# First stage of a two-block network on one core: loads chained tile by tile, four loads moved behind them, mean squares closed per stream, scale slices placed one feature tile later

## The chip, the core and the metric

The kernel runs on one core of one Trainium2 chip. The metric is the device time of one launch in microseconds; lower is better. TensorE is the matrix engine, VectorE (DVE in the rows) and ScalarE (ACT) do elementwise work, GpSimd (POOL) does little here, SyncE (SP) issues nearly all loads. Sixteen DMA engines carry what any of the queues issues.

## The reference, cut to what matters

The function is a chain of two network blocks on 256 tokens of width 1024, with a context of 256 more tokens. Only the beginning of the first block is touched by the change:

```python
mod = jax.nn.silu(c) @ w_mod[i] + b_mod[i]
sh1, sc1, ga1, sh2, sc2, ga2 = [m[:, None, :] for m in jnp.split(mod, 6, axis=-1)]
mod_c = jax.nn.silu(c_ctx) @ w_mod[i] + b_mod[i]
...
hc = modulate(ctx, g_mix[i], csh1, csc1)     # rmsnorm(ctx) * g * (1 + scale) + shift
hx = modulate(x, g_mix[i], sh1, sc1)
y, yc = mlstm_mixer(hx, hc, ...)             # k = hc, hx @ w_in[:, keys], gates, then q, v, o
```

So: root-mean-square norm of ctx and of x over their rows, a scale and a shift per feature that come from two vector-by-matrix products (one condition vector for each stream), and then the products of both streams with the key and gate columns. Everything after that (the rest of the first mixer, a gated convolution, and a second block with four feed-forward layers, a gated linear attention and a latent attention) is left as it is.

## The kernel before

A program lists all instructions in an order of the author's; a planner then places them on the engines by priority (earlier in the program goes first, `urgent()` raises a priority) as their inputs become ready in its own estimate. `behind(op, first)` tells it to place `op` behind `first` on the queue, without a semaphore. Buffers come from pools; a load whose buffer isn't free waits at its issue, and what stands behind it on that queue waits as well.

The first stage, `start()`, works on feature tiles f = 0 to 7 of 128 features each.

- Ahead of it, SP's queue loads ccol (both condition vectors as columns), ident, ctx into xc (two halves of 128 tokens), x (two halves), wsc0 (the scale weights of tile 0) and cols (small vectors), lines 138 to 151.
- `cond_rows()` (L482) spreads the condition vectors over all partitions by TensorE (L488), for the sums against the shift weights; VectorE and ScalarE copy the result (L490).
- Lines 499 to 505: the mean squares of the four halves, the first 512 columns of each on ScalarE (`mean_square`, L324), the second 512 on VectorE (L504). Line 507 closes all four at once and `rsqrt_half` (L295 to 319) takes the inverse root by integer arithmetic and three steps, ten small VectorE instructions with line 507.
- `features(h)` (L510): normalises columns h*512 to h*512+511 of both streams into xn (L517 on VectorE, L521 on ScalarE), turns them over on TensorE (L528) and copies the result to xt (L530). `features(0)` is urgent; `features(1)` stands after tile 0's products.
- `vectors(f)` (L545): loads wsc (scale weights of tile f, 512 KB) and wsh (shift weights, 512 KB), loads and splits the key and gate columns a_kg of the tile (`unit`, 320 KB; whi on ScalarE L236, wlo on VectorE L237), multiplies wsc with ccol on TensorE into pg (L556), sums wsh against each condition row on VectorE (`ttr`, L256) and closes gsc (scale, L563) and shc (shift, L566). From f = 3 on the pg matmuls stand behind the last product of tile f-3 (L558).
- `keys(f)` (L568): u = xt * gsc + shc for both streams on ScalarE (L572), split into a high and a low half (L245 and L576 on ScalarE, L246 on VectorE), and thirty-odd matmuls (L585 to L592) that accumulate keys and gates over the tiles. For tile 0 the high parts of both streams go through one matmul each (L585).

The program calls `vectors(0)`, `vectors(1)`, then for each f `vectors(f+1)` and `keys(f)`.

The scale weights and the high halves share eight buffers, the shift weights and the low halves another eight, and the raw loads five. Four more loads are called far later in the program, on POOL's queue: mpos (L664, 128 KB), gain (`row_load`, L400, 512 KB after it is spread over the partitions), gout (L1020, 128 KB) and perm (L1173, 64 KB). POOL's queue is empty at the start and their buffers are free, so the planner has put them first there.

## Time and profile before

| | us |
|---|---|
| median of three runs | 1430.35 |
| lowest and highest of the three | 1429.79, 1434.51 |
| the profiled execution | 1434.38 |
| its span, first to last instruction | 1432.6 |

Engines over the span: TensorE busy 1380.0 us (96%), VectorE 1113.9 us (78%), ScalarE 720.5 us (50%). The times in the rows are microseconds from the start of the span; "idle before <-" names what an engine waited for. [...] Ends of matmuls are modelled, so neighbours overlap in the rows.

### The profile page before, as it was taken

The numbers are of one execution on the slowest core, as the hardware profiler recorded it, in microseconds if no ns is written. First come the engines' busy times: TensorE is split into PE (matmuls) and PEld (weight loads), VectorE is DVE, ScalarE is ACT, GpSimd is POOL, SyncE is SP. The second block draws the span as 40 slices with busy tenths as digits, with TensorE's granted clock in tenths as the row PEclk, the third lists the DMA queues.
The fourth block names the chain that finished last, engine by engine and source line by source line (L and its number), as shares of the span: only waits on it lengthen the run. The fifth ranks groups of instructions, "written<-read, shape, count | busy, mean of one in ns | idle before, by whom it ended". The sixth has DMA issues, their size and how long they took to land.

```text
span 1432.6 us, 22526 instructions
## 1 busy us (share of the span) xinstructions
PE 1380.0 (96%) x8425; PEld 1204.0 (84%) x8425; DVE 1113.9 (78%) x2115; ACT 720.5 (50%) x1188; POOL 18.2 (1%) x42
## 2 busy tenths in 40 slices
PE   6999999999989999999999999999999999899997
PEld 6978877899978999878678999879999776789996
DVE  6887788898688888689788888698878786756563
ACT  4634764545354545566454545554554666644451
POOL 1000000000000000000000000000000000000000
PEclk8999999999999999999999999999999999999999
DMA  8576446797528999568548999469889472366750
GB/s 330 203 265 234 162 151 234 264 323 272 184 96 290 336 340 345 196 222 290 187 154 289 341 335 344 147 202 334 317 310 333 138 253 80 121 198 205 276 170 30
DMA packets 94943, 340.24 MB, mean 238 GB/s; under 512 B 10928, under 2 KB 11248, under 8 KB 94832
## 3 DMA queue, kind: packets, MB, share of 16 engines
q1 hardware_dynamic: 92736, 332.47, 65.6%
q0 software_dynamic: 2096, 6.33, 1.5%
q8 instruction: 66, 1.08, 0.3%
q14 instruction: 45, 0.37, 0.1%
HBM read 337.67 MB, written 1.08 MB: 236 GB/s over the span
## 4 chain that ended last, share of the span: by engine, by line
PE 70%; DVE 11%; DMA 10%; ACT 4%; issue 3%; SPq 0%; DVEq 0%; ACTq 0%; POOLq 0%
PE mm L250 12%; PE mm L252 11%; PE mm L251 11%; PE acc L252 8%; PE acc L250 8%; PE acc L251 8%; DMA raw<-in_cond_w_dram 3%; DVE wlo L237 3%; DVE gjunk L256 2%; PE acc L733 2%; ACT whi L236 1%; ACT ajunk L324 1%; PE pt L347 1%; PE pg L556 1%; DMA row<-d 1%
## 5 line engine op out<-in xcount | busy, mean ns | idle before, releaser
L237 DVE TENSOR_TENSOR wlo<-raw,whi 128x1024 fp32r<-128x1024 f32 (+1 forms) x385 | 462.5, 1207 | 109.6 <-ACT whi L236 106.7
L236 ACT CAST whi<-raw 128x1024 fp32r<-128x1024 f32 (+1 forms) x385 | 395.7, 1038 | 277.1 <-PE mm L251 79.5
L250 PE MATMUL mm<-u_hi,whi 128*128 128x256 f32 x1384 | 388.5, 281 | 0.2 <-DVE hf L831 0.2
L251 PE MATMUL mm<-u_lo,whi 128*128 128x256 f32 x1384 | 386.6, 279 | 0.0
L252 PE MATMUL mm<-u_hi,wlo 128*128 128x256 f32 x1384 | 386.5, 279 | 0.0
L250 PEld LDWEIGHTS mm<-u_hi,whi 128*128 128x128 f32 x1384 | 260.0, 188 | 4.4 <-DVE hf L831 0.6
L251 PEld LDWEIGHTS mm<-u_lo,whi 128*128 128x128 f32 x1384 | 259.3, 187 | 3.3
L252 PEld LDWEIGHTS mm<-u_hi,wlo 128*128 128x128 f32 x1384 | 260.1, 188 | 0.0
L256 DVE CUSTOM_DVE_ANT_0 gjunk<-raw,c 128x1024 bf16<-128x1024 f32 x192 | 234.3, 1221 | 24.1 <-DMA raw<-in_cond_w_dram 16.5
L250 PE MATMUL acc<-whi,hh 128*128 128x512 f32 x388 | 153.6, 398 | 4.5 <-ACT hh L245 4.5
L252 PE MATMUL acc<-whi,hl 128*128 128x512 f32 x388 | 153.3, 397 | 0.3 <-DVE hl L246 0.3
L251 PE MATMUL acc<-wlo,hh 128*128 128x512 f32 x388 | 152.5, 393 | 0.5 <-DVE wlo L237 0.5
L252 PEld LDWEIGHTS acc<-whi,hl 128*128 128x128 f32 x388 | 73.4, 189 | 17.4 <-DVE hl L246 0.7
L250 PEld LDWEIGHTS acc<-whi,hh 128*128 128x128 f32 x388 | 72.9, 188 | 17.5 <-ACT hh L245 5.0
L252 PE MATMUL acc<-whi,u_lo 128*128 128x512 f32 (+1 forms) x216 | 86.7, 403 | 0.5 <-DVE u_lo L246 0.5
L250 PE MATMUL acc<-whi,u_hi 128*128 128x512 f32 (+1 forms) x216 | 86.5, 401 | 0.0
L251 PE MATMUL acc<-wlo,u_hi 128*128 128x512 f32 (+1 forms) x216 | 86.4, 400 | 0.0
L251 PEld LDWEIGHTS acc<-wlo,hh 128*128 128x128 f32 x388 | 73.2, 189 | 14.2 <-DVE wlo L237 1.3
L251 PE MATMUL mm<-wlo,u_hi 128*128 128x512 f32 x144 | 57.3, 398 | 0.0
L250 PE MATMUL mm<-whi,u_hi 128*128 128x512 f32 x144 | 57.2, 397 | 0.0
L252 PE MATMUL mm<-whi,u_lo 128*128 128x512 f32 x144 | 57.0, 397 | 0.0
L946 ACT ACTIVATE sg<-mm 128x256 f32<-128x256 f32 x64 | 24.3, 380 | 59.6 <-PE mm L252 59.5
(734 smaller groups left out, 1998.6 us busy)
## 6 DMA issues: line engine op xcount, KB each, us to landing
raw<-in_cond_w_dram SPq DMA_DIRECT2D x144, 512.0 KB, 5.2
raw<-in_gu_ws_dram SPq DMA_DIRECT2D x128, 512.0 KB, 5.0
raw<-in_dn_dram SPq DMA_DIRECT2D x88, 512.0 KB, 4.9
raw<-in_gu_dram SPq DMA_DIRECT2D x48, 512.0 KB, 4.3
raw<-in_w_mod_dram SPq DMA_DIRECT2D x32, 512.0 KB, 4.3
raw<-in_f_down_dram SPq DMA_DIRECT2D x22, 512.0 KB, 4.6
raw<-in_f_gate_dram SPq DMA_DIRECT2D x18, 512.0 KB, 4.9
raw<-in_a_vo_dram SPq DMA_DIRECT2D x16, 512.0 KB, 5.1
```

Of the source, the lines that this page charges most:

```text
L236: o1 = S.copy(hi[:, :n], r[:, :n])
L237: o2 = V.tensor_tensor(out=lo[:, :n], in0=r[:, :n], in1=hi[:, :n].bitcast(F32), op=ALU.subtract)
L250: T.matmul(ps, lhsT=lh, rhs=rh, start=first, stop=False)
L251: T.matmul(ps, lhsT=lh, rhs=rl, start=False, stop=False)
L252: T.matmul(ps, lhsT=ll, rhs=rh, start=False, stop=last)
L256: return V.tensor_tensor_reduce(out=junk, in0=r, in1=vec, scale=1.0, scalar=0.0, op0=ALU.mult, op1=ALU.add, accum_out=dst)
L324: mark["ms"] = S.activation(out=junk[:, :src.shape[-1]], in_=src, func=AF.Square, scale=float(2 * width) ** -0.5, accum_out=dst)
L347: T.transpose(pt[:, k, :], src[:, (h * 4 + k) * 128:(h * 4 + k + 1) * 128], ident)
L556: o = T.matmul(pg, lhsT=wsc[:, k * 128:k * 128 + 128], rhs=ccol[:, k, :], start=(k == 0), stop=(k == 7))
L733: T.matmul(np_[:, 0:257], lhsT=w[:, d, s, :], rhs=vt[s][:, h, :], start=(i == 0), stop=(i == len(tiles) - 1))
L946: S.activation(out=sg, in_=ps[:, 0:256], func=AF.Silu)
```

## The change

Six edits, all in the first stage but for the four loads.

1. wsh of tile 0 is loaded with wsc of tile 0, ahead of cols.
2. The loads of the later tiles run in a chain: each key slice, wsc and wsh is placed behind the one before on SP's queue (`load`, `mark["loads"]`), in the order a_kg 0, wsc 1, wsh 1, a_kg 1, and so on.
3. mpos, gain, gout and perm go to SP's queue, behind the last load of that chain (`late`).
4. The mean squares are closed for each stream by itself, ctx first, and ctx's first features follow at once (`stats`, then `features(0, ...)`, both urgent). Instead of one closing chain for four values there are two for two values.
5. For the first half of x's tokens both column halves are squared on ScalarE; for the second half of x's tokens VectorE's square is placed behind ctx's scaling (`xn0`).
6. The pg matmuls of tile f stand behind the last product of tile f-2 rather than f-3, from f = 2 on.

```diff
--- before.py
+++ after.py
@@ -140,12 +140,14 @@
     nc.sync.dma_start(out=ident, in_=a["ident"])
     x = const.tile([128, 2, D], F32, name="x")
     wsc0 = hi_p.tile([128, 1024], F32, name="wsc", tag="w")
+    wsh0 = lo_p.tile([128, 1024], F32, name="wsh", tag="w")
     xc = ar.tile([128, 2, D], F32, name="xc", tag="A")
     for t in range(2):
         nc.sync.dma_start(out=xc[:, t, :], in_=a["ctx"][t * 128:(t + 1) * 128])
     for t in range(2):
         nc.sync.dma_start(out=x[:, t, :], in_=a["x"][t * 128:(t + 1) * 128])
     nc.sync.dma_start(out=wsc0, in_=a["w_sc"][0])
+    nc.sync.dma_start(out=wsh0, in_=a["w_sh"][0])
 
     cols = const.tile([128, LINE(NCOLS)], F32, name="cols")
     nc.sync.dma_start(out=cols[:, :NCOLS], in_=a["cols"])
@@ -177,9 +179,9 @@
     mod2 = const.tile([128, 20, 8], F32, name="mod2")
 
 
-    def raw_load(src):
+    def raw_load(src, load=nc.sync.dma_start):
         r = raw_p.tile([128, 1024], F32, name="raw", tag="raw")
-        nc.sync.dma_start(out=r[:, :src.shape[-1]], in_=src)
+        load(out=r[:, :src.shape[-1]], in_=src)
         return r
 
     pins, bg_pins, mark = [], [], {}
@@ -224,9 +226,9 @@
     def first(stage, i, src, slot=None):
         return early.pop((stage, i)) if (stage, i) in early else unit(src, slot)
 
-    def unit(src, slot=None):
+    def unit(src, slot=None, load=nc.sync.dma_start):
         n = src.shape[-1]
-        r = raw_load(src)
+        r = raw_load(src, load)
         if slot is None:
             hi = hi_p.tile([128, 1024], F32R, name="whi", tag="w")
             lo = lo_p.tile([128, 1024], F32R, name="wlo", tag="w")
@@ -395,9 +397,13 @@
         G.dma_start(out=r, in_=d.rearrange("a b -> (a b)").partition_broadcast(128))
         return r
 
-    def row_load(src):
+    def late(out, in_):
+
+        behind(nc.sync.dma_start(out=out, in_=in_), mark["loads"])
+
+    def row_load(src, load=G.dma_start):
         r = row_p.tile([128, D], F32, name="row", tag="row")
-        G.dma_start(out=r[:, :src.shape[-1]], in_=src.partition_broadcast(128))
+        load(out=r[:, :src.shape[-1]], in_=src.partition_broadcast(128))
         return r
 
     def acc_ps(t, h):
@@ -495,67 +501,81 @@
         V.tensor_scalar(out=b1, in0=col("b_mod", 8, 8), scalar1=1.0, scalar2=None, op0=ALU.add)
         xt = [ar.tile([128, 8, 256], F32, name=f"xt{i}", tag="BC"[i]) for i in range(2)]
         ss = sm.tile([128, 2, 4], F32, name="ss4", tag="ss4", bufs=1)
+        r2 = []
         cond_rows()
-        for i, src in ((0, xc), (1, x)):
+
+        def stats(i, src):
+
             for t in range(2):
                 j = i * 2 + t
                 mean_square(src[:, t, 0:512], ss[:, 0, j:j + 1], D)
+                if j == 2:
+                    mean_square(src[:, t, 512:1024], ss[:, 1, j:j + 1], D)
+                    continue
                 junk = wk.tile([128, D], BF16, name="gjunk", tag="gjunk", bufs=1)
-                V.tensor_tensor_reduce(out=junk[:, 0:512], in0=src[:, t, 512:1024], in1=src[:, t, 512:1024], scale=0.5 / D,
-                                       scalar=0.0, op0=ALU.mult, op1=ALU.add, accum_out=ss[:, 1, j:j + 1])
+                o = V.tensor_tensor_reduce(out=junk[:, 0:512], in0=src[:, t, 512:1024], in1=src[:, t, 512:1024],
+                                           scale=0.5 / D, scalar=0.0, op0=ALU.mult, op1=ALU.add, accum_out=ss[:, 1, j:j + 1])
+                if i:
+                    behind(o, mark["xn0"])
+            js = slice(i * 2, i * 2 + 2)
+            V.scalar_tensor_tensor(out=ss[:, 0, js], in0=ss[:, 0, js], scalar=0.5 * EPS, in1=ss[:, 1, js], op0=ALU.add, op1=ALU.add)
+            r2.append(rsqrt_half(ss[:, 0, js], 2))
+
+        def features(h, i, src):
+
+            xn = wk.tile([128, 2, 512], F32, name="xn", tag="xn")
+            for t in range(2):
+                w, r = src[:, t, h * 512:h * 512 + 512], r2[i][:, t:t + 1]
+                if t == 0:
+                    o = V.tensor_scalar_mul(out=xn[:, t, :], in0=w, scalar1=r)
+                    if h == 0:
+                        mark["xn"] = mark["xn0"] = o
+                else:
+                    o = S.activation(out=xn[:, t, :], in_=w, func=AF.Copy, scale=r)
+                    if h == 0:
+                        mark["xa"] = o
+            for t in range(2):
+                pt = (acc_ps(i, t) if h == 0 else mm_ps() if t == 0 else
+                      ps_tr.tile([128, 512], F32, name="pt", tag="tc")).rearrange("p (k n) -> p k n", k=4)
+                for k in range(4):
+                    T.transpose(pt[:, k, :], xn[:, t, k * 128:k * 128 + 128], ident)
+                dst = xt[i][:, h * 4:h * 4 + 4, t * 128:t * 128 + 128]
+                (S.copy if t else V.tensor_copy)(dst, pt)
+
+        streams = ((0, xc), (1, x))
         with urgent():
-            V.scalar_tensor_tensor(out=ss[:, 0, :], in0=ss[:, 0, :], scalar=0.5 * EPS, in1=ss[:, 1, :], op0=ALU.add, op1=ALU.add)
-            r4 = rsqrt_half(ss[:, 0, :], 4)
-
-        def features(h):
-
-            for i, src in ((0, xc), (1, x)):
-                xn = wk.tile([128, 2, 512], F32, name="xn", tag="xn")
-                for t in range(2):
-                    w, r = src[:, t, h * 512:h * 512 + 512], r4[:, i * 2 + t:i * 2 + t + 1]
-                    if t == 0:
-                        o = V.tensor_scalar_mul(out=xn[:, t, :], in0=w, scalar1=r)
-                        if h == 0:
-                            mark["xn"] = mark["xn0"] = o
-                    else:
-                        o = S.activation(out=xn[:, t, :], in_=w, func=AF.Copy, scale=r)
-                        if h == 0:
-                            mark["xa"] = o
-                for t in range(2):
-                    pt = (acc_ps(i, t) if h == 0 else mm_ps() if t == 0 else
-                          ps_tr.tile([128, 512], F32, name="pt", tag="tc")).rearrange("p (k n) -> p k n", k=4)
-                    for k in range(4):
-                        T.transpose(pt[:, k, :], xn[:, t, k * 128:k * 128 + 128], ident)
-                    dst = xt[i][:, h * 4:h * 4 + 4, t * 128:t * 128 + 128]
-                    (S.copy if t else V.tensor_copy)(dst, pt)
-
-        with urgent():
-            features(0)
+            for st in streams:
+                stats(*st)
+                features(0, *st)
         gsc = const.tile([128, 8, 2], F32, name="gsc")
         shc = const.tile([128, 8, 2], F32, name="shc")
         gp = mm_ps()
         kp = []
         kgu = {}
 
-        def kg_unit(f):
+        def load(out, in_):
+
+            o = nc.sync.dma_start(out=out, in_=in_)
+            if "loads" in mark:
+                behind(o, mark["loads"])
+            mark["loads"] = o
+
+        def vectors(f):
+
+            wsc, wsh = wsc0, wsh0
+            if f:
+                wsc = hi_p.tile([128, 1024], F32, name="wsc", tag="w")
+                load(wsc, a["w_sc"][f])
+                wsh = lo_p.tile([128, 1024], F32, name="wsh", tag="w")
+                load(wsh, a["w_sh"][f])
             if f < 1:
                 pin(1, 4)
-            kgu[f] = unit(a["a_kg"][f])
-
-        def vectors(f):
-
-            wsc = wsc0
-            if f:
-                wsc = hi_p.tile([128, 1024], F32, name="wsc", tag="w")
-                nc.sync.dma_start(out=wsc, in_=a["w_sc"][f])
-            wsh = lo_p.tile([128, 1024], F32, name="wsh", tag="w")
-            nc.sync.dma_start(out=wsh, in_=a["w_sh"][f])
-            kg_unit(f)
+            kgu[f] = unit(a["a_kg"][f], load=load)
             pg = ps_tr.tile([128, 2], F32, name="pg", tag="tr")
             for k in range(8):
                 o = T.matmul(pg, lhsT=wsc[:, k * 128:k * 128 + 128], rhs=ccol[:, k, :], start=(k == 0), stop=(k == 7))
-                if k == 0 and f >= 3:
-                    behind(o, mark["kg"][f - 3])
+                if k == 0 and f >= 2:
+                    behind(o, mark["kg"][f - 2])
             o = ttr(wsh, cc, shc[:, f, 0:1])
             if f == 0:
                 behind(o, mark["xn0"])
@@ -599,7 +619,8 @@
                 vectors(f + 1)
             keys(f)
             if f == 0:
-                features(1)
+                for st in streams:
+                    features(1, *st)
         return gp, kp
 
     gp, kp = start()
@@ -661,7 +682,7 @@
             gc = const.tile([128, 6, 64], F32, name="gc", tag="cc")
             V.tensor_copy(gc, gt_ps[:, 0:384].rearrange("p (s n) -> p s n", s=6))
         mpos = const.tile([128, 2, 128], F32, name="mpos", tag="cb")
-        G.dma_start(out=mpos, in_=a["mpos"])
+        late(out=mpos, in_=a["mpos"])
 
 
         qT = ar.tile([128, H, 256], F32, name="qT", tag="Q")
@@ -685,7 +706,7 @@
                 dst = vt[i][:, g * 2:g * 2 + 2, 0:256]
                 (S.copy if i % 2 else V.tensor_copy)(dst, flat[i].rearrange("p (h n) -> p h n", h=2))
                 site()
-        gain = row_load(a["a_gain"])
+        gain = row_load(a["a_gain"], late)
         so = scratch(0).rearrange("p (t n) -> p t n", t=2)
         for g in range(2):
             units = [unit(a["a_vo"][2 + g, j]) for j in range(4)]
@@ -1017,7 +1038,7 @@
         vt = scratch(0).rearrange("p (t n) -> p t n", t=2)
         rt = scratch(1).rearrange("p (t n) -> p t n", t=2)
         gout = hp.tile([128, 256], F32, name="gout", tag="gout", bufs=1)
-        G.dma_start(out=gout, in_=a["gl_gout"].partition_broadcast(128))
+        late(out=gout, in_=a["gl_gout"].partition_broadcast(128))
         units, got = {}, {}
 
         def vr(i, t):
@@ -1170,7 +1191,7 @@
         V.tensor_scalar(out=kf, in0=kf, scalar1=-1.0, scalar2=1.5707963267948966, op0=ALU.mult, op1=ALU.add)
         S.activation(out=mla.C, in_=kf, func=AF.Sin)
         mla.perm = const.tile([128, 128], F32, name="perm")
-        G.dma_start(out=mla.perm, in_=a["perm"])
+        late(out=mla.perm, in_=a["perm"])
 
     def rope(src, dst, tokens, rp):
```

## Rows read from the trace of the kernel before

**Rows 1.** The page: the chain that ended last, share of the span by engine.

```profile
PE 70%; DVE 11%; DMA 10%; ACT 4%; issue 3%; SPq 0%; DVEq 0%; ACTq 0%; POOLq 0%
```

**Rows 2.** Windows: stretch, length, busy us of each engine (instructions), PEclk, DMA share, GB/s.

```profile
14.20:20.90 6.70, 6.35 (x30) 6.38 (x31) 4.68 (x19) 2.50 (x5) 0.00 (x0) 0.50 1.03 403
20.90:24.40 3.50, 2.65 (x24) 2.48 (x22) 3.50 (x9) 3.25 (x7) 0.00 (x0) 0.99 1.02 408
24.40:31.20 6.80, 5.53 (x21) 5.14 (x22) 6.59 (x13) 4.21 (x9) 0.00 (x0) 0.50 1.00 391
31.20:68.60 37.40, 37.40 (x324) 37.36 (x324) 29.85 (x61) 20.96 (x41) 1.70 (x4) 1.00 0.57 201
```

**Rows 3.** Timeline of TensorE: start, us, instruction, [idle before]; the stage's first and last.

```profile
14.55 3.55 PE L556 MATMUL pg<-ccol,wsc 128*128 128x2 f32 x16 [5.29 <-DMA wsc<-in_w_sc_dram]
17.96 3.41 PE L528 MATMUL acc<-ident,xn 128*128 128x128 f32 x16
25.67 0.79 PE L585 MATMUL acc<-u,whi 128*128 128x512 f32 x1 [2.12 <-ACT u L576]
...
68.37 0.28 PE L592 MATMUL mm<-u_hi,wlo 128*128 128x256 f32 x1
```

**Rows 4.** Timeline of VectorE, from x's last square to the shift of tile 0.

```profile
13.26 0.69 DVE L504 CUSTOM_DVE_ANT_0 gjunk<-x 128x512 bf16<-128x512 f32 x1
...
14.08 0.17 DVE L507 SCALAR_TENSOR_TENSOR ss<-ss 128x4 f32<-128x4 f32 x1
...
16.25 0.49 DVE L517 TENSOR_SCALAR xn<-xc,r 128x512 f32<-128x512 f32 x1
16.66 0.48 DVE L517 TENSOR_SCALAR xn<-x,r 128x512 f32<-128x512 f32 x1
...
19.70 1.22 DVE L256 CUSTOM_DVE_ANT_0 gjunk<-wsh,cc 128x1024 bf16<-128x1024 f32 x1
...
20.84 0.69 DVE L530 COPY xt<-acc 128x512 f32<-128x512 f32 x1
21.44 1.22 DVE L256 CUSTOM_DVE_ANT_0 gjunk<-wsh,c 128x1024 bf16<-128x1024 f32 x1
...
22.65 0.82 DVE L237 TENSOR_TENSOR wlo<-raw,whi 128x640 fp32r<-128x640 f32 x1
23.39 0.22 DVE L566 TENSOR_SCALAR shc<-shc,cols 128x2 f32<-128x2 f32 x1
```

**Rows 5.** Timeline of ScalarE: its squares of the second halves, and their waits.

```profile
8.78 0.63 ACT L324 ACTIVATE ajunk<-xc 128x512 bf16<-128x512 f32 x1 [2.04 <-DMA xc<-in_ctx_dram]
...
13.21 0.63 ACT L324 ACTIVATE ajunk<-x 128x512 bf16<-128x512 f32 x1 [0.55 <-DMA x<-in_x_dram]
```

**Rows 6.** DMA queues from 6 to 9 us: packets, MB, share of sixteen engines' time.

```profile
q0 software_dynamic: 129, 0.46, 69.4%
q1 hardware_dynamic: 128, 0.46, 37.4%
```

**Rows 7.** Windows with and without POOL's loads, columns as in rows 2.

```profile
6.00:9.00 3.00, 3.00 (x24) 3.00 (x22) 1.47 (x4) 0.94 (x3) 0.00 (x0) 1.00 1.07 307
...
12.00:15.00 3.00, 0.45 (x3) 0.48 (x3) 2.75 (x10) 1.86 (x5) 0.00 (x0) 0.86 1.03 406
```

**Rows 8.** Timeline of all engines, 43.5 to 51 us: from one pg to the next.

```profile
43.74 1.84 PE L556 MATMUL pg<-ccol,wsc 128*128 128x2 f32 x16
...
45.62 0.28 DVE L563 TENSOR_SCALAR gsc<-pg,b,cols 128x2 f32<-128x2 f32 x1 [2.09 <-PE pg L556]
...
47.37 0.40 ACT L245 CAST u_hi<-u 128x256 fp32r<-128x256 f32 x1
...
49.04 1.84 PE L556 MATMUL pg<-ccol,wsc 128*128 128x2 f32 x16
```

**Rows 9.** Waits of SP's queue, 24 to 66 us: total us, times, longest us.

```profile
SPq L550 <- PE mm L592: 12.8, 2, 7.2
```

**Rows 10.** Waits of TensorE from 68 us to the end, columns as in rows 9.

```profile
PE acc L250 <- ACT hh L245: 4.5, 2, 4.2
```

## What the change should do to the time

> **What bounds the kernel now.** I read five views in this order. First the page's chain of work that ended last: 70% of it lies on TensorE [rows 1]. So time is lost only where TensorE has nothing to do or runs at its low clock, and a gain anywhere else is no gain. Second, the windows by stage [rows 2]. From 31.2 to 68.6 us TensorE is busy 37.40 of 37.40 us at granted clock 1.00; between 14.2 and 31.2 us it runs at 0.50 or stands still. The loss that the change can touch lies ahead of the first key product, the matmul of L585 that starts at 25.67 us after 2.12 us of waiting for ScalarE's u [rows 3]; the last one ends at 68.65 us (68.37 + 0.28).
>
> Third, what leads to 25.67 us. Two things take turns. Loads: ScalarE waits for xc until 8.78 us and for x until 13.21 us [rows 5]. VectorE after that: all four mean squares are closed at once at 14.08 us, the inverse root takes until 16.25 us, and then come the scaling, two long sums against wsh, two copies of transposes, a split of weights and the small shift at 23.39 us [rows 4]. From the end of the shift (23.61 us) to the first matmul are 2.06 us of ScalarE (u, its casts).
>
> Fourth, the DMA. In 6 to 9 us the POOL queue holds 69.4% of the sixteen engines' time for 0.46 MB, SP's queue 37.4% for the same 0.46 MB [rows 6], and the total falls to 307 GB/s; in 12 to 15 us, with POOL's loads gone, it is 406 GB/s [rows 7]. POOL's loads are mpos, gain, gout and perm, none of which the first 68 us use. Fifth, the later waits of TensorE: the longest kind after 68 us, of 4.5 us, is for hh [rows 10].
>
> **The change part by part.**
>
> *Four loads behind the chain.* mpos 128, gain 512, gout 128 and perm 64 KB are 0.85 MB. They leave the stretch in which ctx and x land. x's last half landed at 13.21 us [rows 5]. Without 0.85 MB at 406 GB/s it lands 2.1 us earlier, and the slow stretch of 3 us at 307 instead of 406 GB/s gives back another 0.3 MB or 0.7 us [rows 7]: 10.4 us. Ends: 13.2 us if SP's queue is no faster alone, 9.4 us if it moves its own bytes from 4 us on without a break. The second half of ctx, at 8.78 us before, lands at about 7.1 us: some 0.7 MB of POOL's bytes, 1.7 us, had gone ahead of it. On SP the four issue behind the last key load, ahead of the a_q loads at worst. Their 2.1 us of transfer are covered by 31.2 to 68.6 us, where the DMA share is 0.57 [rows 2]; a_q's products come after 80 us. Without that cover the price would be 2.1 us.
>
> *Chain of loads, wsh0 early.* Key slice, wsc, wsh now leave tile by tile, each behind the one ahead. wsc0 and wsh0 still stand behind x and land some 1.3 us apart (512 KB at 406 GB/s), about 11.6 and 12.9 us, before VectorE asks for them. Cost nothing. What is queued behind a waiting issue is every later weight load; SP already waits 12.8 us in two waits for matmuls to free wsc's buffer [rows 9], and now key slices stand behind such a wait. Their lead is several feature tiles, so I take nothing here either.
>
> *Statistics per stream.* VectorE loses one half-row square (0.82 us from its start at 13.26 to the next step at 14.08 [rows 4]), which ScalarE takes over in time that it spent waiting for x. The square that stays is put behind ctx's scaling; behind it on VectorE stands x's closing chain, and the path below counts it in that place. VectorE gains a second closing chain: ten small instructions, 14.08 to 16.25 us, 2.17 us [rows 4]. I sum the new path on VectorE with start-to-start times of rows 4. ctx half 7.1; square 0.82, so 7.9; chain 2.17, so 10.1; scaling 0.41 (16.25 to 16.66 us, the next one's start), so 10.5. A copy of the condition row, priced as the copy of rows 4 (20.84 to 21.44), 0.60: 11.1. x is there by then (10.4). Square of x 0.82: 11.9. Chain 2.17: 14.1. Copy of ctx's transposes 0.60: 14.7. Scaling 0.41: 15.1. Then what stood before too: the long sums, 19.70 to 20.84 and 21.44 to 22.65, 2.35; x's transposes 0.60; scale slice 0.28 [rows 8]; split 22.65 to 23.39, 0.74; shift 0.22: 4.2 in all, 19.3 us. ScalarE's 2.06 us: **21.35 us instead of 25.67, 4.3 us earlier.** Ends: 6.3 us earlier if the two copies and the split fall outside the path; 2.3 us if x still lands at 13.2 us (13.2 + 0.82 + 2.17 + 0.41 + 0.60 + 4.2 + 2.06 = 23.4). So the second chain costs VectorE time, but the first of the two runs while x is still on its way; without that cover it would cost 2.17 us.
>
> *Scale slices one tile later.* pg of tile f now stands behind the products of tile f-2 at the earliest. In the middle of the stage it stands there already: pg at 43.74 us, to 45.58, then 3.5 us of products, then pg at 49.04 us. The first pg's scale is taken at 45.62 and the cast of u_hi ends at 47.77 us, 2.2 us after pg and 1.3 us ahead of the next one [rows 8]. While VectorE waited for a later pg, the gemv sums, splits and casts of lo behind it on its queue would wait too, and ScalarE's u with them; I take nothing, since the 1.3 us are there.
>
> *TensorE's clock.* [...] Granted clock 0.50 reigned from 14.2 us although TensorE was busy 6.35 of 6.70 us, it rose, and fell again at 24.4 us after a stretch busy 2.65 of 3.50 us [rows 2]. [...] The changed stage also has gaps before the products, so I take the same loss; ends: 2.8 us better, 1 us worse. [...]
>
> *The rest of the kernel.* From the first product on TensorE is packed: 5.53 us busy up to 31.2, then 37.40 of 37.40 us [rows 2], while VectorE has 7.5 us to spare in the latter. So 4.3 us at the start is 4.3 us at 68.65 us. After that nothing is removed or added. Instructions are put in order by a planner, and a few may stand otherwise; no row shows such a shift, so I bound it by one wait of the longest kind, 4.2 us of the 4.5, gained or lost [rows 10], and take zero, since work, loads and buffers there are unchanged.
>
> Sum: 1434.38 us for the profiled execution (span 1432.6 and 1.8 around it) minus 4.3 is 1430.1. That execution lies 4.03 us above the median of the three, 1430.35, near their highest; I take the difference off the median: **1426.0 us** (1430.35 - 4.32).
>
> **The rivals.**
>
> [...]
>
> *VectorE or the loads hold the start.* The POOL loads may not be what held x, or small work may pile up on VectorE, which is busy 6.59 of 6.80 us from 24.4 us on [rows 2]. Then the start moves 2.3 us: 1428.0. This is also the case that the change doesn't do what it says: the loads move and x lands as before.
>
> *Given back later.* The products start earlier and a wait of 4.2 us appears downstream: 1430.2.
>
> *Slower: the scale slice comes too late.* pg now can't run ahead, so each tile has the 3.5 us of the products before it to get scale, u and casts done, which need 2.2 us [rows 8]. It decides as soon as more than 1.3 us of other VectorE work stands ahead of the scale. With both long sums and one split ahead (2.35 + 0.74 = 3.1 us) TensorE stands 1.8 us in each of six tiles, 10.8 us; less the 4.3 won, 6.5 us slower: 1436.8. Against it: in rows 8 the scale follows pg at once.
>
> [...]
>
> **How the numbers follow.** Forecast 1426.0: 0.50. Clock 1423.2: 0.20. Start held, 1428.0: 0.15. Given back, 1430.2: 0.05. Slower, 1436.8: 0.10. A measurement of this kernel tells about 0.3%, 4.3 us, from no change: faster ends at 1426.06. The forecast lies on that line, with ends of 2 us on both sides (1424.0 to 1428.0); I give 0.28 of its 0.50 to faster. With the clock's 0.20 that is 0.48 faster; 0.22 + 0.15 + 0.05 = 0.42 within; 0.10 slower. The range leaves out the slower rival and the far ends of front and clock together (6.3 + 2.8 us): 1421.5 to 1431.0.
>
> **What the changed profile would show.** x landing near 10.4 us, read from ScalarE's and VectorE's waits; two closing chains on VectorE, the first over by 10.5 us; the first L585 matmul near 21.4 us; the last key product near 64.3 us with no more gaps between; POOL's queue nearly empty before 12 us. The prediction is wrong if the first product starts early but the last doesn't, if TensorE waits for u from tile 1 on, or if the shift at 64 us isn't found at the end.

## The result, and the profile after

The changed kernel is slower. Medians on the same chip: 1445.36 us (7 runs, 1440.61 to 1451.82) against 1435.01 us for the kernel before (7 runs, 1429.79 to 1437.96), ratio 1.0079 with a 95% interval of 1.0052 to 1.0107. The forecast was 1426.0 us, the range ended at 1431.0. The profiled execution has a span of 1444.3 us against 1432.6, so 11.7 us are to be found.

First the front. Timeline of the changed kernel, all engines, from ctx's last square to the first key product (start, us, engine, line, instruction, [idle before it <- what ended it]); it answers [rows 3 to 5]:

```profile
6.34 0.63 ACT L326 ACTIVATE ajunk<-xc 128x512 bf16<-128x512 f32 x1 [0.62 <-DMA xc<-in_ctx_dram]
...
10.14 0.48 DVE L530 TENSOR_SCALAR xn<-xc,r 128x512 f32<-128x512 f32 x1
...
14.14 0.48 DVE L530 TENSOR_SCALAR xn<-x,r 128x512 f32<-128x512 f32 x1
...
18.35 0.22 DVE L586 TENSOR_SCALAR shc<-shc,cols 128x2 f32<-128x2 f32 x1
...
18.49 3.58 PE L576 MATMUL pg<-ccol,wsc 128*128 128x2 f32 x16 [1.53 <-DVE gsc L583]
18.61 1.09 ACT L592 ACTIVATE u<-xt,shc,gsc 128x256 f32<-128x256 f32 x2 [0.40 <-DVE shc L586]
...
22.68 1.63 PE L605 MATMUL acc<-u,whi 128*128 128x512 f32 x3
```

Up to the shift all came as forecast or sooner: it ends at 18.57 us instead of 23.61. The first product, though, starts at 22.68 us, 3.0 us before the 25.67 of [rows 3] and not 4.3. What stands ahead of it on TensorE is the second tile's pg. It waits for the first tile's scale to free its buffer and then takes 3.58 us at a granted clock of 0.50; four transposes follow it (from 21.93 us).

Then the key stage. Windows of the changed kernel (stretch, length, busy us of PE, PEld, DVE, ACT, POOL with instructions, PEclk, DMA share, GB/s): the whole stage, two stretches in it, and two behind it.

```profile
22.68:71.55 48.87, 48.16 (x341) 45.94 (x339) 34.49 (x70) 20.70 (x42) 1.70 (x4) 0.87 0.51 180
42.00:44.00 2.00, 2.00 (x11) 1.87 (x12) 1.97 (x6) 0.75 (x2) 0.00 (x0) 0.65 1.00 371
44.00:46.00 2.00, 2.00 (x11) 2.00 (x11) 2.00 (x4) 0.00 (x0) 0.00 (x0) 0.50 0.99 325
71.55:76.56 5.01, 0.00 (x0) 0.00 (x1) 2.75 (x4) 4.91 (x7) 0.00 (x0) 1.00 0.85 303
76.56:80.10 3.54, 3.38 (x7) 2.21 (x8) 2.57 (x3) 3.53 (x4) 0.00 (x0) 0.52 0.76 251
```

The same window of the kernel before, from its first key product to the end of its last:

```profile
25.67:68.65 42.98, 42.98 (x344) 42.55 (x345) 35.17 (x70) 23.93 (x46) 1.70 (x4) 0.94 0.62 226
```

The stage grew from 42.98 to 48.87 us, and the last product ends at 71.55 instead of 68.65 us. The granted clock is 0.50 or 1.00 in nearly every half microsecond of the stage, so by an estimate from its mean of 0.87, 12.7 of the 48.87 us ran at 0.50 (48.87 x 0.13 / 0.50). A pg takes 3.58 us at 0.50 (18.49 us) and 1.84 us at 1.00 (34.28 us), so if TensorE alone set the pace there, that cost about half, 6.4 us; before it was 2.8 us (the 5.5 us from 25.67 to 31.2 us at 0.50 [rows 2]). So by this estimate the clock makes 3.6 of the 5.9 us in this execution. Idle time is only 0.7 us by the profile; the rest is not resolved, since the ends of matmuls are modelled. Behind the last product TensorE then stands still for 5.01 us, which it did not before. After that the granted clock falls twice more (0.52 from 76.56 to 80.10 us above, and 0.50 from 93.80 to 97.20 us), where the kernel before had 1.00 from 31.2 to 105 us; by the same estimate that is up to 3.4 us. Together: 3.0 us won in front, 5.9 + 5.0 + 3.4 us lost, 11.3 of the 11.7 us.

What changed inside a tile is seen in the timeline of the changed kernel from one pg to the next; it answers [rows 8]:

```profile
34.28 1.84 PE L576 MATMUL pg<-ccol,wsc 128*128 128x2 f32 x16
...
36.16 0.28 DVE L583 TENSOR_SCALAR gsc<-pg,b,cols 128x2 f32<-128x2 f32 x1 [3.63 <-PE pg L576]
...
37.02 1.22 DVE L258 CUSTOM_DVE_ANT_0 gjunk<-wsh,cc 128x1024 bf16<-128x1024 f32 x1
...
38.29 1.23 DVE L258 CUSTOM_DVE_ANT_0 gjunk<-wsh,c 128x1024 bf16<-128x1024 f32 x1
...
39.44 0.82 DVE L239 TENSOR_TENSOR wlo<-raw,whi 128x640 fp32r<-128x640 f32 x1
...
40.18 0.22 DVE L586 TENSOR_SCALAR shc<-shc,cols 128x2 f32<-128x2 f32 x1
40.43 1.09 ACT L592 ACTIVATE u<-xt,shc,gsc 128x256 f32<-128x256 f32 x2 [5.54 <-DVE shc L586]
```

VectorE stands 3.63 us for pg, and only then does the two sums, the split and the shift of that tile (the fourth, f = 3). So u starts 4.3 us after pg has ended (36.12 to 40.43). In the kernel before, the split (40.09 us) and both sums (40.82 and 42.30 us) of the tile of [rows 8] are done ahead of its scale of 45.62 us, and the shift follows the scale at once:

```profile
40.09 0.82 DVE L237 TENSOR_TENSOR wlo<-raw,whi 128x640 fp32r<-128x640 f32 x1
...
42.30 1.22 DVE L256 CUSTOM_DVE_ANT_0 gjunk<-wsh,c 128x1024 bf16<-128x1024 f32 x1
...
45.81 0.22 DVE L566 TENSOR_SCALAR shc<-shc,cols 128x2 f32<-128x2 f32 x1
```

There u starts at 46.07 us, 0.5 us after its pg. In the changed kernel the work behind the scale did not wait for its data: the shift slice of that tile had left SP's queue at 13.15 us and its key slice at 14.42 us. It is the place in VectorE's order that is late. Waits from 24 to 70 us (total us, times, longest), first of the kernel before, then of the changed one:

```profile
ACT u L572 <- DVE shc L566: 17.3, 7, 3.9
DVE gsc L563 <- PE pg L556: 5.4, 4, 2.1
```

```profile
ACT u L592 <- DVE shc L586: 25.0, 6, 5.5
DVE gsc L583 <- PE pg L576: 12.6, 5, 3.6
```

Last, the loads that the work behind the stage needs: a_q and the first a_vo slices, on SP's queue, four each (start of the first, us until the last has left; before, the first a_q slice has a row of its own). First of the kernel before, then of the changed one, with two instructions of ScalarE and the product of TensorE that ends the 5 us:

```profile
45.08 0.38 SPq L182 DMA_DIRECT2D raw<-in_a_q_dram  x1
...
46.02 6.77 SPq L182 DMA_DIRECT2D raw<-in_a_q_dram  x3
...
57.72 8.72 SPq L182 DMA_DIRECT2D raw<-in_a_vo_dram  x4
```

```profile
41.92 17.34 SPq L184 DMA_DIRECT2D raw<-in_a_q_dram  x4
66.17 5.54 SPq L184 DMA_DIRECT2D raw<-in_a_vo_dram  x4
...
71.88 0.68 ACT L645 ACTIVATE gb<-mm,cols 64x512 f32<-64x512 f32 x1
...
75.48 1.03 ACT L238 CAST whi<-raw 128x1024 fp32r<-128x1024 f32 x1
...
76.56 1.10 PE L252 MATMUL acc<-whi,v 128*128 128x512 f32 x2 [5.01 <-ACT whi L238]
```

The value slices leave 8.5 us later, and TensorE waits for the first of them to be cast. But the first had landed 3.3 us after it left, at 69.5 us, ahead of the last key product; its cast starts at 75.48 us, since ScalarE does the gates' first activation, the last query slice's cast, a table load and another activation before it. In the kernel before, three such casts stand at 63.32 us, ahead of that work. So the 5.0 us are an order on ScalarE, not a load that is still under way.

Against the kernel before, equal instructions stand 5.0 us earlier at 21 us on VectorE, 3.2 us later at the gates (69 us), and on TensorE 11.8 us later at 104 us and 12.5 us later at 150 us. Behind that it wanders between 10 and 16 us, with 12.5 us at the end: nearly all of the loss arises ahead of 110 us.

### The profile page after: what moved, and what is told of

The parts are those of the page before. It is cut to its first block, busy times and chain, and to the rows that moved or that the text cites. A ratio compares the mean times of both kernels' runs of the same rounds, so it can differ in the third digit from the quotient of the medians.

```text
span 1444.3 us, 22527 instructions
## 1 busy us (share of the span) xinstructions
PE 1390.8 (96%) x8425; PEld 1211.6 (84%) x8425; DVE 1116.6 (77%) x2124; ACT 721.7 (50%) x1190; POOL 16.0 (1%) x38
## 4 chain that ended last, share of the span: by engine, by line
PE 74%; DVE 12%; DMA 6%; ACT 5%; issue 3%; DVEq 0%; ACTq 0%; SPq 0%
PE mm L252 13%; PE mm L254 13%; PE mm L253 12%; PE acc L254 9%; PE acc L252 9%; PE acc L253 9%; DMA raw<-in_cond_w_dram 3%; DVE wlo L239 3%; PE acc L754 2%; DVE gjunk L258 1%; ACT whi L238 1%; ACT ajunk L326 1%; PE pt L349 1%; PE pg L576 1%; DVE u L360 1%
## 5 line engine op out<-in xcount | busy, mean ns | idle before, releaser
L254 PEld LDWEIGHTS acc<-whi,u_lo 128*128 128x128 f32 x216 | 40.6, 188 | 11.5 <-issue 2.8
```

The source lines that it names most:

```text
L254: T.matmul(ps, lhsT=ll, rhs=rh, start=False, stop=last)
```

## The experiments

Theory A: the chain did it. It leaves the loads' bytes as they were but turns round VectorE's order in each tile, and it holds back the loads that follow. Theory B: the scale slices placed one tile later (edit 6) did it, by the mechanism of my slower rival. Theory C: the four late loads keep SP's queue busy where key slices should leave. Ratios are to the kernel before on the same chip, with 95% intervals.

| kernel | median us | before us | ratio | first key product | last one ends | a_vo leaves |
|---|---|---|---|---|---|---|
| after | 1445.36 | 1435.01 | 1.0079 (1.0052 to 1.0107) | 22.68 | 71.55 | 66.17 |
| 1 no chain | 1431.51 | 1434.46 | 0.9975 (0.9961 to 0.9989) | 21.09 | 66.12 | 55.21 |
| 2 pg back | 1445.44 | 1434.46 | 1.0075 (1.0050 to 1.0100) | 23.92 | 74.48 | 69.09 |
| 3 sums first | 1436.68 | 1434.46 | 1.0019 (1.0005 to 1.0033) | 22.93 | 66.54 | 60.97 |
| 4 late loads back | 1448.72 | 1434.46 | 1.0093 (1.0064 to 1.0123) | 26.83 | 72.67 | 67.28 |
| 5 chain alone | 1449.12 | 1432.69 | 1.0111 (1.0081 to 1.0140) | 28.00 | 76.51 | 71.13 |
| 6 key slices free | 1433.36 | 1432.69 | 1.0000 (0.9985 to 1.0015) | 20.60 | 64.81 | 53.93 |
| 7 pg's own buffer | 1429.61 | 1432.69 | 0.9974 (0.9958 to 0.9989) | 22.18 | 65.37 | 54.46 |
| 8 closed together | 1430.71 | 1432.69 | 0.9972 (0.9952 to 0.9993) | 21.88 | 64.39 | 53.47 |
| 9 late loads alone | 1429.58 | 1434.48 | 0.9970 (0.9952 to 0.9989) | 21.88 | 64.03 | 53.10 |
| 10 8 with 7 | 1430.54 | 1434.48 | 0.9969 (0.9952 to 0.9987) | 21.46 | 65.04 | 54.12 |
| 11 sums behind | 1445.18 | 1433.68 | 1.0076 (1.0050 to 1.0102) | 22.55 | 82.17 | 62.18 |

**1. The changed kernel without the chain.**

```diff
             o = nc.sync.dma_start(out=out, in_=in_)
-            if "loads" in mark:
-                behind(o, mark["loads"])
             mark["loads"] = o
```

> The changed kernel without the chain: the loads of w_sc, w_sh and the key slices are no longer placed behind one another; all else stays. Theory A (the chain makes the planner put each tile's two long sums, its split and its shift behind the scale slice on VectorE, so u starts 4.3 us after its pg instead of 0.5 us, TensorE waits and its clock falls): the last key product ends near 65 us instead of 69.8, VectorE's idle time before the scale slices falls from 15.7 us to under 8 us, and the time comes out 10 to 16 us below the changed kernel, at or below the kernel before. Theory B (scale slices one tile later): the time stays within 3 us of the changed kernel. Theory C (loads on SP come too late from the four late ones): stays as well.

The whole loss is gone, with a little gain over the kernel before. The value slices leave at 55.21 us, and no 5 us wait follows.

**2. Scale slices two tiles ahead again.**

```diff
-                if k == 0 and f >= 2:
-                    behind(o, mark["kg"][f - 2])
+                if k == 0 and f >= 3:
+                    behind(o, mark["kg"][f - 3])
```

> The changed kernel with the pg matmuls of tile f behind the products of tile f-3 again. Theory A: nothing changes in the order on VectorE, the time stays within 3 us of the changed kernel. Theory B: the stage runs as before, the time falls by 8 us or more.

No difference from the changed kernel; VectorE's wait for pg is 14.2 us in five waits. Theory B falls.

**3. The chain kept, the sums put ahead of the scale by hand.**

```diff
-            ttr(wsh, c1, shc[:, f, 1:2])
+            o2 = ttr(wsh, c1, shc[:, f, 1:2])
             o = V.tensor_scalar(out=gsc[:, f, :], in0=pg, ...
             behind(o, mark["xn"])
+            if f >= 2:
+                behind(o, o2)
```

> The changed kernel with the chain of loads kept as it is, but each scale slice from tile 2 on is placed behind the tile's second long sum on VectorE. Theory A, with the order on VectorE as the mechanism: u starts within 1.5 us of its pg, the last key product ends 3 to 5 us earlier than in the changed kernel, and the time falls by 4 to 12 us. Rival (the chain's loads themselves land too late, order or not): VectorE then waits for w_sh instead, and the time doesn't fall by more than 2 us. If a part of the loss is that the a_vo loads leave at 66 instead of 58 us because key slices hold the raw buffers longer, that part (some 5 us of TensorE waiting for whi at 71 to 76 us) stays.

Windows and waits of this kernel (the wait is one of 24 to 105 us):

```profile
30.00:45.00 15.00, 15.00 (x131) 15.00 (x131) 11.20 (x24) 5.43 (x12) 0.00 (x0) 1.00 0.74 259
45.00:60.00 15.00, 15.00 (x132) 15.00 (x132) 11.34 (x23) 7.14 (x15) 0.00 (x0) 1.00 0.45 165
```

```profile
PE acc L252 <- ACT whi L238: 5.0, 1, 5.0
```

TensorE is busy all of 30 to 60 us at clock 1.00, and the last product ends 5.0 us earlier than with the chain's own order. But the 5.0 us behind the stage stay, with the value slices leaving at 60.97 us. So there are two losses: the order within the tile, the larger part (1.0079 to 1.0019), and what follows the stage, the rest (1.0019 to the 0.9975 of experiment 1). Here too the first value slice is there in time (left at 60.97 us, landed 3.4 us later) and its cast starts at 70.46 us.

**4. The four loads on POOL's queue again, all else as changed.**

```diff
-        late(out=mpos, in_=a["mpos"])
+        G.dma_start(out=mpos, in_=a["mpos"])
```

(gain, gout and perm likewise.)

> The changed kernel with mpos, gain, gout and perm on POOL's queue at the start again. Theory A: the first stage starts later by what their 0.85 MB cost the loads of ctx and x, x's last half lands 1.5 to 3 us later, the first key product comes 0 to 3 us later, and the time is 0 to 3 us above the changed kernel. Theory C (they delay loads behind them on SP): the time falls by 3 us or more.

Theory C falls: the kernel is no faster. The first product moves 4.1 us back, so these loads are the front's gain.

The run also tells order and clock apart. Window of the stage from where its clock has risen, and its waits from 24 to 70 us:

```profile
30.80:72.67 41.87, 39.82 (x328) 38.60 (x326) 30.66 (x61) 19.88 (x41) 1.70 (x4) 1.00 0.52 176
```

```profile
ACT u L592 <- DVE shc L586: 24.7, 7, 5.6
DVE gsc L583 <- PE pg L576: 12.7, 6, 3.6
```

VectorE's order and waits are those of the changed kernel, but the clock is 1.00 to the end of the stage, and TensorE stands 2.05 us. One pg follows another after 5.7 us (44.16 to 49.88), as it does in the changed kernel where the clock stays at 1.00 (34.28 to 39.99), and after 5.3 us with the sums first (45.17 to 50.48). Where the clock falls in between, it is 7.2 us (39.99 to 47.24 in the changed kernel, at 0.50 from 43 to 46 us). So the order costs 0.4 us per tile at clock 1.00, and each fall of the clock in the stage, which this execution does not have, adds some 1.5 us. With 1443.57 us it is the fastest of the four executions of this kernel; the others lie at 1447.99 to 1452.45. Behind the stage TensorE waits 5.0 us here too, and the clock falls (0.51 from 75.10 to 82.00 us).

**5. The kernel before with the chain alone.**

```diff
+        def load(out, in_):
+            o = nc.sync.dma_start(out=out, in_=in_)
+            if "loads" in mark:
+                behind(o, mark["loads"])
+            mark["loads"] = o
...
-            kgu[f] = unit(a["a_kg"][f])
+            kgu[f] = unit(a["a_kg"][f], load=load)
...
-                nc.sync.dma_start(out=wsc, in_=a["w_sc"][f])
+                load(wsc, a["w_sc"][f])
...
-            nc.sync.dma_start(out=wsh, in_=a["w_sh"][f])
+            load(wsh, a["w_sh"][f])
```

> The kernel before with the chain alone: the loads of scale slice, shift slice and key slice of the eight tiles each stand behind the one of them issued before, and nothing else is changed (loads of the front, statistics, scale slices two tiles ahead, four loads on the Pool queue as before). Theory A (the chain alone turns VectorE's order round, so that each tile's two long sums, split and shift stand behind the tile's scale, and the scale waits for TensorE's pg): the first key product stays at about 25.7 us, from the third tile on u starts some 4 us after its pg has ended, the last key product comes 5 to 9 us later than the 68.65 of before, the granted clock falls below 1.00 somewhere between 31 and 75 us, and the time is 8 to 14 us above before, 1442 to 1449 us. Theory D (the chain does harm only together with the scale slices moved a tile later and the statistics split): the time stays within 4 us of before and the sums of a tile stay ahead of its scale.

Its waits from 24 to 70 us:

```profile
ACT u L579 <- DVE shc L573: 24.4, 6, 7.0
DVE gsc L570 <- PE pg L563: 12.9, 7, 3.3
```

The chain needs no other edit to do harm: 16 us, a little more than the 14 at the upper end of theory A. The first product, which I had left at 25.7 us, comes at 28.00: here too the second tile's pg (3.41 us from 24.40 us) now stands ahead of it.

**6. Key slices free, scale and shift slices chained.**

```diff
-            kgu[f] = unit(a["a_kg"][f], load=load)
+            kgu[f] = unit(a["a_kg"][f])
```

> The changed kernel with the eight key slices' loads out of the chain; the scale and shift slices stay chained. Theory A2 (it is the key slices' place in the chain that does the harm: with a key slice landing only behind its tile's shift slice its split cannot run tiles ahead, and it also holds the raw buffers that the query slices wait for): the long sums stand ahead of the scale again, TensorE runs at a granted clock of 1.00 from about 31 us to the last key product at 65 to 67 us, the value slices' loads leave near 55 us instead of 66, and the time is as without any chain, 1428 to 1434 us. Rival (the chained scale and shift slices do it alone): as after, 1443 to 1447 us, with u 4 us behind its pg. Rival in between (order repaired, buffers still held): as with the sums first, 1435 to 1438 us.

Its waits from 24 to 70 us:

```profile
ACT u L592 <- DVE shc L586: 15.7, 6, 3.0
DVE gsc L583 <- PE pg L576: 6.3, 5, 1.4
```

One argument takes the loss away. Both waits are those of the kernel without a chain (15.7 and 6.3 us there too), and the value slices leave earlier still. The small gain of experiment 1 doesn't appear (1.0000 against 0.9975, intervals that overlap); whether the chained scale and shift slices cost that much is not settled. Within the chain it is the key slices that do the harm. Free, four of them leave at the front of SP's queue and three more by 20 us, and from the middle of the stage on each is split a tile ahead of its use. Chained, five have left by 18.65 us and then one per tile (29.38, 35.10, 40.93 us), and the split stands on VectorE with the sums of its own tile, behind the scale. No key slice was late for its split: the last left at 40.93 us and is split at 65.32. Why the planner places the splits so can't be read from the runs, since its own estimate is not in them.

**7. No chain, and a PSUM buffer of its own for the second tile's pg.**

```diff
-            pg = ps_tr.tile([128, 2], F32, name="pg", tag="tr")
+            pg = ps_tr.tile([128, 2], F32, name="pg", tag="tc" if f == 1 else "tr")
```

> The changed kernel without the chain, and the second tile's pg in a PSUM buffer of its own, so that it need not wait for the first tile's scale. If pg of the second tile, which stands ahead of the first key product on TensorE (18.65 to 21.23 us without the chain), is what holds that product back, pg runs before 17 us and the first product starts when the first cast of u is done, 20.5 us, instead of 21.09: 0.6 us earlier, at most 1.5 us if the clock stays up for it. The time is then 0 to 1.5 us below that of the kernel without the chain. If another wait takes its place (VectorE's split of u), the first products stand still for as long, and the time is the same.

A miss. pg no longer waits for the scale, but for its weights, 18.05 to 21.59 us, and the first product comes at 22.18 us, later than with one buffer. The time is the same as in 1. Its weights land little before the buffer came free (18.65 us in 1), and it takes 3.54 instead of 2.58 us, about the 3.58 us that a pg took at a granted clock of 0.50 in the changed kernel.

**8. No chain, statistics closed once for both streams, as before the change** (and all four second halves squared on VectorE).

```diff
-            js = slice(i * 2, i * 2 + 2)
-            V.scalar_tensor_tensor(out=ss[:, 0, js], ...
-            r2.append(rsqrt_half(ss[:, 0, js], 2))
...
+            V.scalar_tensor_tensor(out=ss[:, 0, :], ...
+            r4 = rsqrt_half(ss[:, 0, :], 4)
+            r2.extend([r4[:, 0:2], r4[:, 2:4]])
```

> The changed kernel without the chain, and the statistics of both streams closed together again, as before the change (with all four second half rows summed on VectorE). The prediction's step: closing by stream takes ctx's half out of x's way and lets x's scaling start about 3 us earlier than it would with one closing behind the last half row. If so, the first key product comes 2 to 3.5 us later than the 21.09 us without the chain, and the time is 0 to 3 us above it (1431 to 1435 us). Rival: x's landing alone sets the front, and closing by stream is worth under 1 us of the first product.

Timeline of this kernel, then of the one with two closings (experiment 1):

```profile
9.79 0.63 ACT L326 ACTIVATE ajunk<-x 128x512 bf16<-128x512 f32 x1 [0.55 <-DMA x<-in_x_dram]
...
13.23 0.48 DVE L522 TENSOR_SCALAR xn<-x,r 128x512 f32<-128x512 f32 x1
...
21.88 0.52 PE L599 MATMUL acc<-u,whi 128*128 128x512 f32 x1 [0.19 <-ACT u L590]
```

```profile
14.29 0.49 DVE L530 TENSOR_SCALAR xn<-x,r 128x512 f32<-128x512 f32 x1
...
21.09 0.77 PE L603 MATMUL acc<-u,whi 128*128 128x512 f32 x1
```

The rival holds. With one closing x's scaling comes 1.06 us sooner, since nothing of ctx stands ahead of it; the first product comes 0.8 us later; the time is the same. Closing by stream bought nothing that can be measured.

**9. The kernel before with the four late loads alone.**

```diff
-            nc.sync.dma_start(out=wsh, in_=a["w_sh"][f])
+            mark["loads"] = nc.sync.dma_start(out=wsh, in_=a["w_sh"][f])
...
+    def late(out, in_):
+        behind(nc.sync.dma_start(out=out, in_=in_), mark["loads"])
...
-        G.dma_start(out=mpos, in_=a["mpos"])
+        late(out=mpos, in_=a["mpos"])
```

(gain, gout and perm likewise.)

> The kernel before with the four later loads alone behind the first stage's loads (mask, gain row, output gain, permutation go from the Pool queue to SP's); statistics, chain, scale slices and the first shift slice as before. If these four loads are the front's whole gain: x's second half is there by 10.5 us, the first key product starts at 21.5 to 22.5 us instead of 25.67, the last key product ends 2.5 to 4 us before the 68.65 of before, and the time is 1 to 4 us below before (ratio 0.997 to 0.9995). Rival (they need the statistics closed by stream or the first shift slice in the front): the first product gains under 2 us and the time stays within 1 us of before.

Timeline and window of this kernel:

```profile
10.00 0.63 ACT L324 ACTIVATE ajunk<-x 128x512 bf16<-128x512 f32 x1 [0.53 <-DMA x<-in_x_dram]
...
13.44 0.48 DVE L521 TENSOR_SCALAR xn<-x,r 128x512 f32<-128x512 f32 x1
...
21.88 0.50 PE L589 MATMUL acc<-u,whi 128*128 128x512 f32 x1 [1.38 <-ACT u L580]
```

```profile
21.88:64.03 42.15, 42.15 (x344) 41.66 (x345) 35.17 (x70) 23.45 (x45) 1.71 (x4) 0.96 0.64 236
```

x is there at 10.0 instead of 13.2 us, the products run from 21.88 to 64.03 us without a gap, and the time falls by 0.3%. Equal instructions stand 4.6 us earlier all through the key stage and 3.3 us at 200 us; behind that the single profile wanders between 2 us later and 3 us earlier. As far as these runs tell, this is the whole of what the change had to give.

**10. Experiment 8 with the edit of 7.**

```diff
-            pg = ps_tr.tile([128, 2], F32, name="pg", tag="tr")
+            pg = ps_tr.tile([128, 2], F32, name="pg", tag="tc" if f == 1 else "tr")
```

> The changed kernel without the chain, with one closing of the statistics for both streams and the second tile's pg in a PSUM buffer of its own: the three edits kept are the first shift slice in the front, the four later loads behind, and the scale slices one tile later. Sought as the fastest form. The front's gain is then as with one closing (first product at 21 to 22 us) and the time 1428 to 1431 us, ratio to before 0.9965 to 0.998. Rival: the front's 3 to 4 us are given back behind the key stage as without the chain (offset back to about 0 at 104 us), ratio 0.998 to 1.000.

The same as 9: five kernels (1, 7, 8, 9, 10) lie at 0.997, and no two of them can be told apart. The smallest edit is 9; it has neither the early shift slice nor the other squares of edit 5.

**11. No chain, and VectorE's order turned round by hand** (`scale()` is the tensor_scalar that reads pg and makes gsc).

```diff
+            if f >= 2:
+                g = scale()
             o = ttr(wsh, cc, shc[:, f, 0:1])
+            behind(o, g if f >= 2 else mark["xn0"])
             o2 = ttr(wsh, c1, shc[:, f, 1:2])
+            if f >= 2:
+                behind(o2, g)
```

> The changed kernel without the chain, in which VectorE's order alone is turned round by hand: from the third tile on the two long sums of a tile stand behind its scale. The loads stay free. Theory A (the order on VectorE is what costs TensorE time in the key stage): VectorE's scale waits over 2 us for its pg per tile, u starts 3 us or more after pg has ended, TensorE stands still or its granted clock falls below 1.00 between 31 and 70 us, and the last key product, near 66 us without the chain, ends 3 to 8 us later; the value slices' loads leave near 55 us as they do without the chain, so that TensorE's 5 us of waiting for their split behind the key stage stays away; time 1433 to 1440 us. Rival (the order costs nothing, all the loss comes from loads that arrive late): the last key product stays at 66 to 67 us, and the time is as without the chain, 1429 to 1433 us.

Windows of this kernel, columns as above, and its waits from 24 to 70 us:

```profile
34.00:36.00 2.00, 0.13 (x2) 0.03 (x1) 2.00 (x6) 0.00 (x0) 0.00 (x0) 1.00 0.08 31
36.00:38.00 2.00, 2.00 (x10) 2.00 (x11) 0.87 (x4) 1.91 (x5) 0.00 (x0) 0.53 0.00 0
...
54.00:56.00 2.00, 2.00 (x12) 2.00 (x11) 0.00 (x0) 0.00 (x0) 0.00 (x0) 0.50 0.90 369
```

```profile
ACT u L597 <- DVE shc L591: 21.7, 5, 9.0
DVE gsc L578 <- PE pg L574: 15.7, 5, 5.6
```

Such an order alone, with free loads, costs as much as the chain did, 11.5 us against the kernel before and more than the 1440 us that I gave as theory A's end. TensorE stands (0.13 of 2.00 us busy), and behind that its clock is granted at 0.53 (36 to 38 us); it is at 0.50 from 50 to 62 us, behind stands between 46 and 50 us (1.62 and 0.94 of 2.00 us busy). The value slices left at 62.18 us, later than I expected, right behind the last key slice's split (61.33 us); the 5 us wait did stay away. The order made by hand is not the chain's in every place (here u_lo too stands behind the sums), so its size is not the chain's share.

## Why the prediction was wrong, point by point

- **Four loads behind the chain: right, and in size.** x's last half was forecast at 10.4 us; ScalarE's square, which waits for it, starts at 9.79 (experiment 8) and 10.0 us (experiment 9). ctx was forecast at 7.1 and its last square starts at 6.34. The front's gain is these loads, as experiments 4 (4.1 us lost without them) and 9 (3.8 us won by them alone) show. From 6 to 9 us both queues moved 0.46 MB each [rows 6], and with POOL's loads later x comes 3.2 us sooner (10.0 instead of 13.2 us, experiment 9). No run put these loads late on POOL's queue or early on SP's, so how much is the place in line and how much the queue (69.4% against 37.4% of the engines' time for the same bytes) is not shown.
- **Statistics per stream: the path was worked out right, but compared with nothing.** x's scaling, forecast at 14.7 to 15.1 us, came at 14.14; the shift's end, forecast at 19.3, at 18.57. The first closing did run while x was on its way, as I had it (7.20 to 10.14 us). But ctx's scaling and a copy of its transposes then stand on VectorE ahead of x's scaling, and one closing, with x there at 10 us, gives that scaling at 13.2 to 13.4 us. The step should have been summed with and without the edit.
- **From the shift to the first product: 2.06 us was the wrong price.** It took 4.1 us (18.57 to 22.68), since the second tile's pg and four transposes stand there. In [rows 3] TensorE waited 2.12 us for u ahead of that product; once u came earlier, whatever else stood ahead on TensorE's queue was late next, and I did not look at what that was.
- **Chain of loads: "Cost nothing" is the step that failed.** I saw that "key slices stand behind such a wait", and took nothing since "their lead is several feature tiles". I asked whether a load would land late, and none of the key slices did (left at 14.42 us, split at 39.44; the last 40.93 and 65.32). What the chain took away was the lead of the split. The order of VectorE's instructions, which the planner makes from when inputs are ready in its estimate, turned: both sums and the split moved behind the scale, between it and the shift. Experiments 1, 5 and 6 show that it is the chain, alone, by the key slices; 3 shows that the order makes the larger part, and 11 that such an order alone can cost as much. The second part, the 5.0 us behind the stage, outlives the order on VectorE (experiment 3) and goes with the key slices' place (6). It is an order too, the first value slice's cast on ScalarE behind the gates' work. The step also missed what the splits hold back: in all thirteen kernels the first value slice leaves within 0.1 us of the end of the last key slice's split (56.88 + 0.82 and 57.72 us before, 65.32 + 0.82 and 66.17 us after). The view of [rows 9] had a row for it that I left out, `SPq L182 <- DVE wlo L237: 15.8, 5, 5.0`: SP's queue waits for splits to free the raw buffers. That the late leaving is why the planner put the cast late was not tried by itself.
- **Scale slices one tile later: "I take nothing" was right** (experiment 2, with the chain in place; without it, 1, which has the edit, and 9, which has not, can't be told apart either). The slower rival named the place and the work, both sums and a split on VectorE (3.1 us) between scale and products, but blamed edit 6; and I gave it 0.10 because "in rows 8 the scale follows pg at once", a row of the old order. Its size was not right either: it had 10.8 us in the stage, where 5.9 came, and nothing behind it, where the 5.0 us wait and the clock came.
- **TensorE's clock: "the same loss" failed too.** By the estimate above 6.4 us against 2.8 in the stage, 3.6 more, and up to 3.4 us behind it, where my end was 1 us worse. No run shows the clock rates from which the 2.8 us of the better end, and with it 1423.2 us, were worked out; in the rows a pg takes 3.55 us at 0.50 [rows 3] and 1.84 us at 1.00 [rows 8], by which the 5.53 us at 0.50 before would have been some 2.7 us shorter at 1.00 (an estimate). In the changed kernel the stage's first 2.8 us ran at 0.50 (22.68 to 25.5 us). In [rows 2] the clock stays at 1.00 all through 31 to 68 us, and I took that for a property of the stage. In experiment 4, with the same order, it stays at 1.00 as well (30.8 to 72.67 us), so the fall is not a fixed part of the loss.
- **The rest passes 1:1: right for the front's gain where nothing else is changed.** In experiment 9 the first product won 3.8 us, the last 4.6 and the time 0.3%. My last key product at 64.3 us is near the 64.03 us of that kernel by luck: its first product came 0.5 us later than my 21.35, and its stage took 42.15 us instead of the 42.98 that I carried over. For the change as a whole the step failed ("no row shows such a shift"): the planner did place instructions otherwise. The bound of 4.2 us for one such wait [rows 10] was near the 5.0 us that came, but I took it as zero and gave it 0.05. It was also misread: the longest kind of wait after 68 us is `PE pt L347 <- DVE u L358: 8.6, 6, 3.6`; 4.2 us is only the longest single one.

## What to carry to other kernels

Where a planner orders instructions by when their inputs are ready, an edge between loads also reorders the engines that use them: ask of each load that is held back which instruction was early because of it, and what that instruction will now stand behind. Do one edit at a time where the edits are independent: the four moved loads alone give all of the gain that can be measured, and the chain costs three to four times as much (4.3 us against 14 to 16). When a wait ahead of a product is shortened, read the whole queue of its engine, for the next thing on it becomes the wait.

## What the runs showed that was not expected

- The granted clock fell in the changed kernel in stretches where the profile has TensorE busy 2.00 of 2.00 us (42 to 46 us above, at 0.65 and 0.50; again near 56 and 63 us, at 0.56 from 56 to 58 and 0.50 from 64 to 66 us), each behind a pg (39.99, 52.94, 60.17 us); the pgs at 34.28 and 47.24 us had no such fall behind them. With the sums first and pgs just as often it stayed at 1.00 from 30 to 60 us, and with the chain's own order in experiment 4 from 30.8 to 72.67 us. In experiment 11 it fell behind plain standstills (0.53 from 36 to 38 us, behind 0.13 of 2.00 us busy). The spread of the changed kernel's runs goes roughly with it: 1440.61 us at a mean granted clock of 0.985, 1451.82 us at 0.979. What tips it in the first case stays open: the changed kernel has short waits for v and u_lo (0.2 and 0.3 us in all from 24 to 70 us) that the kernel before has not, but experiment 4 stands too (2.05 us) without such a fall in the stage, and ends of matmuls are modelled. No run here took the short waits away by themselves.
- pg's sixteen matmuls have two columns each and still take 1.84 us at clock 1.00 and 3.58 us at 0.50. At the front, where the clock was 0.50 (14.20 to 20.90 us before [rows 2], 18.49 to 22.07 us in the changed kernel), a small product of this kind is worth looking for ahead of a large one.
